# A hybrid attention block on one core: the steps at the seam to the feed-forward part from one table, another block order of the output projection, and local score products over all 128 rows

## The chip, the cores and the metric

The kernel runs on one core of one Trainium2 chip. The metric is the device time of one execution in microseconds (us), as the median of several runs. Lower is better.

## What is computed

One decoder layer on 1024 tokens of width 1024, all in float32. Cut to what matters here:

```python
h = rmsnorm(x, mix_norm_g)
qa, ka, va, q_lat, kv_lat, k_r, g_a, g_b = split(h @ w_in)
o_a = swa_sink_attention(rope(qa), rope(ka), va, sinks)   # 8 heads, 2 kv heads, window 128
o_b = mla_attention(...)                                  # 8 heads, causal, latent q and kv
y = sigmoid(g_a) * (o_a @ w_o_swa) + sigmoid(g_b) * (o_b @ w_o_mla)
x = x + y @ w_out                                         # the output projection
h = rmsnorm(x, ffn_norm_g)
x = x + (silu(h @ w_gate) * (h @ w_up)) @ w_down          # d_ff = 2816
return rmsnorm(x, final_norm_g)
```

## The kernel before

**Products.** Every float32 product is made of three products of a rounded high part and the low rest of each operand (`mm3`, L252 to L258: high by high, high by low, low by high). So each operand is split first: ScalarE copies the high part (`split`, L249), VectorE subtracts it from the source and keeps the rest (L250). The large products use a seven-product block scheme (Strassen-Winograd): the operands are cut into 2 x 2 blocks, some products take sums of blocks, and the results are put together from the seven products. The block sums of weights are made by GpSimd.

**Stages.** The input projection and local (windowed) attention with the gate products between them; latent attention; the gated mix of both (`mix_b`, L1537); the output projection (`X_ORDER`, L1804 to L1870); the gate and up products of the feed-forward part (`Seven`, L783, run 154 times); the down product; the last norm.

**Local scores** (`sw_scores`, L975 to L987). The tile `qs` holds for each of two head pairs and each of two heads 128 rows: 64 rows of the high part of q and 64 rows of its low rest. `khd` holds the keys twice, in rows 0 to 63 and in rows 64 to 127, as a high and as a low tile. A product with the high keys runs over all 128 rows and so adds high and low part of q. A product with the low keys runs over 64 rows alone, rows 0 to 63 for one head (`j = 0`) and rows 64 to 127 for the other (L985). A step has eight such products: two high, two pairs of low ones, two high. There are 16 steps.

**Latent attention** is ordered by a planner (`Plan`, L95) that picks the next step of each engine by estimated times and ranks (`RANK`, L1245).

**The output projection and the seam.** Seven products `q` in the order 1, 2, 6, 7, 5, 4, 3, each over four row blocks `t` of 128 tokens. Products 1, 2, 5, 3 add up in one set of PSUM banks, 6, 7, 4 in another. After each one `xo_done` (L1808) adds the banks to the rows of `x` that are due. Product 4 is the last that rows 0 to 511 (blocks 0 to 3) need, product 3 the last for rows 512 to 1023 (blocks 4 to 7). For each block then follow: the sum of squares (`row_sum`, ScalarE and GpSimd), the scaled row `xn` (`row_norm`, VectorE), eight transposes to the tile `tp` (`next_h`, `to_ps`), and the split tiles of the normed block. The feed-forward part takes them as blocks `b11`, `b21` (from blocks 0 to 3), `b22` (from 4 to 7) and as the block sums `t1` to `t4` (`to_h` L1666, `rest`, `late_split` L1794), each as a high (`t1h`) and a low tile (`t1l`). In `to_h` and `rest` the tile `t` holds two of these sums, and `hraw` the raw blocks and then the other two. GpSimd does one subtraction of `hraw`, the low part of `t3` and the low part of `t4` for each of blocks 4 to 7.

**The feed-forward products** run by pairs `j` of weight columns, products `q`, and matrix `m` ("g" for gate, "u" for up); a list `head` puts (0,1), (0,2), (1,1), (1,2) first, then the products 6, 7, 5, 4, 3 of pair 0 and of pair 1, because 6 and 7 need `t2` and `t3`, 5 needs `t1` and 4 needs `t4`. Each run (`run`, L861) is 12 matmuls of 512 columns. `prep` (L836) splits a weight block into `wl`; `mix` (L822) makes the weight sums `sm` on GpSimd, three operations for each matrix, and `prep` of product 7 one more (`a12 - s1`).

From product 4 of the output projection until 14 weight blocks are prepared (L1844 to L1911) the instructions of PE, VectorE, ScalarE and GpSimd stand in the order of the code; behind that a scheduler orders them. `wd_out` (L1746) makes block sums of `w_down` on GpSimd and stores them, one call for each pair `j`; for j = 0 and 1 it is called after product 5 of that pair.

Of the kernel before, what the change touches and what calls it, by code (L numbers as in the profile page):

```python
# [8 lines left out]
F32 = mybir.dt.float32  # L9
# [169 lines left out]
def hybrid_block_kernel(  # L179
# [603 lines left out]
    class Seven:  # L783


        def __init__(self, pairs, ms, load, done, ahead, load_at, mix_at, head=(), at=None, scale=None, scale_at=(), piece=4):
# [17 lines left out]
            self.piece = piece  # L804
            self.raws, self.sums, self.left, self.acc, self.tmp = {}, {}, {}, {}, {}

# [10 lines left out]
        def part(self, j, m, kh, f):  # L817
            self.load_part(j, kh)
            self.scale_part(j, kh)
            return self.raws[(j, kh)][m][:, :, f]  # L820

        def mix(self, j, eng=None, m=None):  # L822

            for m in self.ms if m is None else (m,):
                if (j, m) in self.sums:
                    continue
                a11, a21, a22 = self.part(j, m, 0, 0), self.part(j, m, 0, 1), self.part(j, m, 1, 1)
                s = self.sums[(j, m)] = U("sm", F32, (P, 2, 4, P))
                eng_, n = (eng, 4) if eng is not None else (nc.gpsimd, self.piece)
                for k in range(0, 4, n):  # L830
                    k = slice(k, k + n)
                    add(s[:, 0, k], a21[:, k], a22[:, k], eng_)
                    sub(s[:, 1, k], s[:, 0, k], a11[:, k], eng_)
                    sub(a21[:, k], a11[:, k], a21[:, k], eng_)

        def prep(self, j, q, m):  # L836
# [5 lines left out]
            if q == 7:  # L842
                a12, s1 = self.part(j, m, 1, 0), self.sums[(j, m)][:, 1]
                for k in range(0, 4, self.piece):
                    k = slice(k, k + self.piece)
                    sub(a12[:, k], a12[:, k], s1[:, k], nc.gpsimd)
# [14 lines left out]
        def run(self):  # L861
# [21 lines left out]
            elif q == 6:  # L883
                add(u2, ps, p1, nc.vector)
            elif q == 7:
                add(u3, ps, p1, nc.vector)
# [9 lines left out]
    def load_gate(j, kh):  # L896
        t = U("wr", F32, (P, 4, 2, P))
# [3 lines left out]
    def scale_gate(j, kh, k, raw):  # L901
        t = raw["g"]
        g = gT[:, 4 * kh + k:4 * kh + k + 1]
        if j == 0:
            nc.vector.tensor_scalar(t[:, k], t[:, k], g, None, op0=ALU.mult)  # L905
        else:
            nc.scalar.activation(t[:, k], t[:, k], AF.Copy, scale=g)
# [67 lines left out]
    def sw_scores(it):  # L975
# [7 lines left out]
        for hp, low in ((0, 0), (0, 1), (1, 1), (1, 0)):  # L983
            for j in range(2):
                r = slice(HD * j, HD * j + HD) if low else slice(0, P)  # L985
                nc.tensor.matmul(scs[j][:, hp, c0:], qs[r, hp, j], khd[g][low][r, kc], start=low == hp,
# [258 lines left out]
    RANK = {'S': -2.38, 'M': -0.6, 'E': -2.86, 'W': -2, 'C': -2, 'V': 3.5, 'O': 1.49, 'A': 2.32, 'Q': -0.9, 'Qm': 2.11, 'Qh': 1.76, 'Ql': 0.5, 'K': -0.3, 'Kh': 0.92, 'Kl': 0.91, 'uh': -1.71, 'ul': -0.83, 'wl': 6.31, 'G': 2.93, 'wh': 0.76, 'bl': 0.9, 'ol': -0.89, 'H': -0.5, 'oh': -0.63}  # L1245
# [279 lines left out]
    proj_steps("oa", 1, NT - 3)  # L1525
# [11 lines left out]
    def mix_b(dc):  # L1537
# [6 lines left out]
        for sh in (1, 0):  # L1544
# [12 lines left out]
    def y_split(q, k):  # L1557
# [4 lines left out]
        src = y_new[0][:, k] if q == 5 else y[k + 4 * (q in (2, 3, 4))][:, half({1: 1, 2: 1, 6: 1, 7: 0, 4: 0, 3: 1}[q])]  # L1562
        split(hi[:, k], lo[:, k], src)

    def y_sums(k):
# [3 lines left out]
        a21, a11, a22, a12 = y[k][:, half(0)], y[k][:, half(1)], y[4 + k][:, half(0)], y[4 + k][:, half(1)]  # L1569
# [83 lines left out]
    raw1 = {}  # L1653
    late = []
# [11 lines left out]
    def to_h(pss, b):  # L1666

        c = b % 4
        if b < 4:
            if b == 0:  # L1670
                new_h("b11")
                new_h("b21")
            raw1[b] = U("hraw", F32, (P, 2, 4, P))
            for kh in range(2):
                split_h(("b11", "b21")[kh], c, pss[kh])
            for kh in range(2):
                nc.scalar.copy(raw1[b][:, kh], pss[kh])
            return
        if b == 4:
            for name in ("b22", "t2", "t3"):  # L1680
                new_h(name)
        r = raw1.pop(c)
        t23 = U("t23", F32, (P, 2, 4, P))
        nc.scalar.copy(t23[:, 1], pss[0])
        sub(r[:, 0], pss[0], r[:, 0], nc.vector)
        sub(t23[:, 0], pss[1], r[:, 0], nc.vector)
        nc.scalar.copy(hq["t2"][0][:, :, blk(c)], t23[:, 0])
        sub(r[:, 1], r[:, 1], t23[:, 0], nc.gpsimd)
        late.append((c, r))

        def rest():
            sub(t23[:, 1], pss[1], t23[:, 1], nc.vector)
            nc.scalar.copy(hq["b22"][0][:, :, blk(c)], pss[1])
            nc.scalar.copy(hq["t3"][0][:, :, blk(c)], t23[:, 1])
            for name, src, eng in (("t2", t23[:, 0], nc.vector), ("b22", pss[1], nc.vector),
                                   ("t3", t23[:, 1], nc.gpsimd)):
                hi, lo = hq[name]
                sub(lo[:, :, blk(c)], src, hi[:, :, blk(c)].bitcast(F32), eng)

        return rest  # L1700

# [3 lines left out]
    def load_w(j, kh):  # L1705
        if j == 0:
            t = [U("wr", F32, (P, 4, 2, P)) for _ in range(2)]
        else:
            v = V("wr", F32, (P, 2, 4, 2, P))
# [5 lines left out]
    def ffn_done(j, m, ps, f, sh, other):  # L1715
# [3 lines left out]
        if other is not None:  # L1719
            add(other, ps, other, nc.vector)  # L1720
# [3 lines left out]
        else:  # L1724
# [4 lines left out]
                {(1, 6): [("load", 2, 0)], (1, 7): [("load", 2, 1)], (1, 5): [("mix", 2)]})  # L1729
# [64 lines left out]
    def late_split(c):  # L1794
        r = late[c][1]
        for i, name in ((0, "t1"), (1, "t4")):
            if c == 0:
                new_h(name)
            split_h(name, c, r[:, i], (nc.vector, nc.gpsimd)[i])
        late[c] = None  # L1800
# [4 lines left out]
    xns = []  # L1805
    rests = []
# [301 lines left out]
```

## Time and profile before

| what | us |
|---|---|
| median of 3 runs | 1347.29 (1346.72 to 1348.11) |
| the profiled execution | 1347.01, of which 1345.2 from the first to the last instruction (the span) |
| TensorE (PE) busy | 1325.4 |
| VectorE (DVE) busy | 927.2 |
| ScalarE (ACT) busy | 653.5 |
| GpSimd (POOL) busy | 591.5 |

A profile lists for each engine when every instruction started and how long it took. PE's matmuls are pipelined: a record of one 512-column product lasts 0.39 us, but the next one starts earlier. Rows of "windows" give, for a stretch of the span, the busy time of PE, of PE's weight loads, of DVE, ACT and POOL with the number of instructions, then the clock that PE was granted (1.00 is full) and the share and rate of the DMA engines. A row of "waits" gives who waited for whom: microseconds in total, how often, the longest.

### The profile page before, as it was taken

Reading aid. Unit: us, or ns where it says so; the run is one execution under the profiler, and the core shown is the slowest. Engines: PE = TensorE matmul, PEld = TensorE weight load, DVE = VectorE, ACT = ScalarE, POOL = GpSimd, SP = SyncE. Lnnn points to the kernel's source line nnn. Section 1 sums busy time; section 2 is a strip of 40 time slices with the busy share of each in tenths; the row PEclk is TensorE's granted clock in tenths of the full one; section 3 lists DMA queues with packets and bytes.
Section 4 is the critical chain, followed back from the end, with each engine's and each line's share of the span. In section 5 each row is a group of like instructions: output and inputs, shape, how many; then the busy total and the mean of one; then the engine's idle time right before and its main releaser. Section 6 shows DMA issues by size and latency. Waiting matters only on the chain. (4 is left out here: it accounts for less than half of the span.)

```text
span 1345.2 us, 18917 instructions
## 1 busy us (share of the span) xinstructions
PE 1325.4 (99%) x6552; PEld 1112.4 (83%) x6552; DVE 927.2 (69%) x1565; ACT 653.5 (49%) x1317; POOL 591.5 (44%) x598
## 2 busy tenths in 40 slices
PE   9999999999999999999998999999999999999997
PEld 6899878878888889888886788888888888888886
DVE  7868767776787786488779675666665654674862
ACT  7433767655577787534365233232222232644352
POOL 1116545454054567230056865756666541022521
PEclk9999999999999999999999999999999999999999
DMA  9454322334200111987042353544443425996504
GB/s 367 159 184 156 116 100 89 99 118 161 90 13 1 47 45 48 328 247 223 1 188 78 132 182 133 208 168 180 166 154 150 164 95 189 368 379 250 172 15 142
DMA packets 78239, 205.39 MB, mean 153 GB/s; under 512 B 8768, under 2 KB 15424, under 8 KB 77504
## 3 DMA queue, kind: packets, MB, share of 16 engines
q1 hardware_dynamic: 76848, 199.99, 42.4%
q0 software_dynamic: 1152, 4.19, 1.6%
q8 instruction: 52, 0.85, 0.3%
q14 instruction: 43, 0.35, 0.1%
q10 hardware_dynamic: 144, 0.00, 0.0%
HBM read 141.24 MB, written 59.77 MB: 149 GB/s over the span
## 5 line engine op out<-in xcount | busy, mean ns | idle before, releaser
L250 DVE TENSOR_TENSOR wl<-wr,wl 128x512 fp32r<-128x512 f32 x150 | 153.4, 1044 | 74.2 <-ACT wl L249 73.9
L250 DVE TENSOR_TENSOR lrv<-lr,lrv 128x1024 fp32r<-128x1024 f32 x77 | 105.1, 1397 | 51.5 <-ACT lrv L249 50.2
L249 ACT CAST lrv<-lr 128x1024 fp32r<-128x1024 f32 x77 | 80.1, 1052 | 96.7 <-PE fd L258 53.9
L256 PE MATMUL fd<-lrv 128*128 128x512 f32 x308 | 119.8, 389 | 0.0
L257 PE MATMUL fd<-lrv 128*128 128x512 f32 x308 | 119.8, 389 | 0.0
L258 PE MATMUL fd<-lrv 128*128 128x512 f32 x308 | 119.8, 389 | 0.0
L261 POOL TENSOR_TENSOR wr<-wr,sm 128x512 f32<-128x512 f32 (+1 forms) x38 | 46.5, 1232 | 116.2 <-DVE wl L250 110.1
L249 ACT CAST wl<-wr 128x512 fp32r<-128x512 f32 x150 | 87.2, 622 | 2.6 <-DVE wr L905 2.0
L250 DVE TENSOR_TENSOR wl<-sm,wl 128x512 fp32r<-128x512 f32 x60 | 53.9, 924 | 45.2 <-ACT wl L249 45.1
L1299 POOL TENSOR_SCALAR p<-p,denb 128x384 f32<-128x384 f32 (+3 forms) x64 | 48.0, 753 | 63.5 <-DVE denb L1295 52.3
L384 POOL TENSOR_SCALAR ms<-ss 128x1 f32<-128x1 f32 x32 | 9.8, 305 | 141.8 <-ACT xn L1820 64.1
L256 PEld LDWEIGHTS fd<-lrv 128*128 128x128 f32 x308 | 57.8, 188 | 12.1
L257 PEld LDWEIGHTS fd<-lrv 128*128 128x128 f32 x308 | 57.8, 188 | 12.0
L258 PEld LDWEIGHTS fd<-lrv 128*128 128x128 f32 x308 | 57.8, 188 | 11.9
L1290 ACT ACTIVATE p<-scb,nmb 128x384 f32<-128x384 f32 (+3 forms) x64 | 47.7, 746 | 23.4 <-DVE nmb L1285 17.4
L1723 ACT ACTIVATE act<-sm 128x512 f32<-128x512 f32 x11 | 7.0, 633 | 105.9 <-DVE sm L264 105.9
L261 DVE TENSOR_TENSOR ptl<-pTb,pth 128x512 fp32r<-128x512 f32 (+2 forms) x96 | 51.1, 551 | 8.1 <-ACT pth L1326 7.4
L1285 DVE CUSTOM_DVE_ANT_0 scb<-scb,mask 128x384 f32<-128x384 f32 (+3 forms) x64 | 48.5, 759 | 8.9 <-PE scb L1272 8.5
L1723 ACT ACTIVATE act<-pu 128x512 f32<-128x512 f32 x22 | 13.9, 633 | 74.4 <-DVE pu L264 74.4
L258 PE MATMUL fa<-t1h,wl 128*128 128x512 f32 x120 | 47.4, 397 | 2.6 <-DVE wl L250 2.6
L258 PE MATMUL fb<-t3h,wl 128*128 128x512 f32 x120 | 47.2, 394 | 1.7 <-DVE wl L250 1.7
L256 PE MATMUL fa<-t1h,wl 128*128 128x512 f32 x120 | 47.9, 399 | 0.0
(363 smaller groups left out, 4341.6 us busy)
## 6 DMA issues: line engine op xcount, KB each, us to landing
lr<-la_d SPq DMA_DIRECT2D x77, 256.0 KB, 5.4
wr<-in_w_gate_dram SPq DMA_DIRECT2D x22, 512.0 KB, 4.3
wr<-in_w_up_dram SPq DMA_DIRECT2D x22, 512.0 KB, 5.3
wd<-in_w_down_dram SPq DMA_DIRECT2D x22, 512.0 KB, 6.8
rb_d<-wd SPq DMA_DIRECT2D x22, 512.0 KB, 2.6
la_d<-sd SPq DMA_DIRECT2D x22, 512.0 KB, 5.4
lr<-rb_d SPq DMA_DIRECT2D x44, 256.0 KB, 5.4
lr<-in_w_down_dram SPq DMA_DIRECT2D x33, 256.0 KB, 5.3
```

Of the source, the lines that this page charges most:

```text
L249: nc.scalar.copy(hi, src)
L250: (eng or nc.vector).tensor_tensor(lo, src, hi.bitcast(F32), op=ALU.subtract)
L256: nc.tensor.matmul(ps, ah, bh, start=first and i == 0, stop=False, skip_group_check=go_on)
L257: nc.tensor.matmul(ps, ah, bl, start=False, stop=False, skip_group_check=go_on)
L258: nc.tensor.matmul(ps, al, bh, start=False, stop=last and i == n - 1, skip_group_check=go_on)
L261: eng.tensor_tensor(out, a, b, op=ALU.subtract)
L384: nc.gpsimd.tensor_scalar(ms, ss, 1.0 / width, EPS, op0=ALU.mult, op1=ALU.add)
L1285: nc.vector.tensor_tensor_reduce(s_, s_, m_, 1.0, -NEG, op0=ALU.add, op1=ALU.min, accum_out=nm)
L1290: nc.scalar.activation(p_, s_, AF.Exp, scale=-1.0, bias=t_.pop(("nm", key)), accum_out=den)
L1299: nc.gpsimd.tensor_scalar(p[:, 0:w], p[:, 0:w], den, 0.0, op0=ALU.mult, op1=ALU.add)
L1723: nc.scalar.activation(dst, src, AF.Silu)
```

## The change

1. **Local scores.** The low products run over all 128 rows too, so that each of the eight products of a step has the same form. They add the product of the low rests, which was left out before.
2. **Output projection.** The order of products is 1, 2, 6, 5, 3, 7, 4, and the halves of rows change roles (also in `y_split`, `y_sums`, `mix_b`): product 3 is now the last that blocks 0 to 3 need, two products before the end, and product 4 the last for blocks 4 to 7. The order of code (not of the scheduler) holds from product 3 on.
3. **The seam from a table.** `SEAM` lists the steps as words: `x30` is product 3 on row block 0, `y` the next operand split of the projection, `s0`, `n0`, `T0` sum of squares, scaled row and transposes of block 0, `h`, `c` and the letters and digits after `T4` single instructions of `to_h` and `rest`, `t`, `v` the splits of `t1` and `t4`, `p` one weight split, `f` one feed-forward run, `m`, `M` weight sums, `D` the DMA of point 4. All subtractions of `hraw`, `t3` and `t4` are on VectorE.
4. **Weight sums.** Signs are turned (`plus=True`), so that the sums of weights are additions. For pair 0 the sum that `prep` of product 7 made on GpSimd (one operation for each matrix) is made by a DMA that adds (`mix_sum(0, 2)`, issued by GpSimd); `mix_load` and the other steps of `mix_sum` are not called.
5. **Layout.** The weight tiles hold the two column blocks of a pair one behind the other, so that a slice of 512 is contiguous (`pairs`, `load_gate`, `load_w`).
6. **Small things.** Ranks for two kinds of steps in the planner of latent attention (`L`, `T`) and one due time; `mix_b` takes the halves in the other order; `wd_out` of pairs 0 and 1 is called after product 5 of pairs 2 and 3.

```diff
     class Seven:
...
-                    sub(s[:, 1, k], s[:, 0, k], a11[:, k], eng_)
-                    sub(a21[:, k], a11[:, k], a21[:, k], eng_)
+                    op(s[:, 1, k], s[:, 0, k], a11[:, k], eng_)
+                    op(a21[:, k], a11[:, k], a21[:, k], eng_)
+        def mix_sum(self, j, step):
+            def plus(dst, src):
+                nc.gpsimd.dma_start(dst, src, accum_op=ALU.add)
...
+                else:
+                    plus(self.part(j, m, 1, 0), s[:, 1])
...
-            if q == 7:
+            if q == 7 and j not in self.by_dma:
...
-                r = slice(HD * j, HD * j + HD) if low else slice(0, P)
-                nc.tensor.matmul(scs[j][:, hp, c0:], qs[r, hp, j], khd[g][low][r, kc], start=low == hp,
+                nc.tensor.matmul(scs[j][:, hp, c0:], qs[:, hp, j], khd[g][low][:, kc], start=low == hp,
                                  stop=low != hp)
...
-    proj_steps("oa", 1, NT - 3)
+    proj_steps("oa", 1, NT - 4)
...
-        for sh in (1, 0):
+        for sh in range(2):
...
+        elif what == "3":
+            sub(t23[c][:, 1], t23[c][:, 1], pss[1], nc.vector)
+        elif what == "i":
+            add(raw1[c][:, 1], raw1[c][:, 1], t23[c][:, 0], nc.vector)
...
+        elif what == "H":
+            sub(hq["t3"][1][:, :, blk(c)], t23[c][:, 1], hq["t3"][0][:, :, blk(c)].bitcast(F32), nc.vector)
+        elif what in "tv":
...
+            split_h(name, c, raw1[c][:, what == "v"], (nc.vector, nc.vector)[what == "v"])
...
-    X_ORDER = (1, 2, 6, 7, 5, 4, 3)
+    X_ORDER = (1, 2, 6, 5, 3, 7, 4)
...
+    SEAM = ("y x30 y s0 n0 x31 y x32 s1 n1 s2 x33 y s3 T0 n2 h0 x70 y m0 c0 T1 n3 x71 h1 c1 T2 x72 h2 c2 m1 "
...
-        if (q, m) == (5 if j < 2 else 2, "u"):
-            if j < HF - 1:
-                wd_out(j)
+        if (q, m) == (2, "u") and 2 <= j < HF - 1:
+            wd_out(j)
+        if (q, m) == (5, "u") and j in (2, 3):
+            wd_out(j - 2)
...
-        return m.reshape(2, 4, P, 2, n, P).transpose(4, 0, 2, 1, 3, 5)
+        return m.reshape(2, 4, P, 2, n, P).transpose(4, 0, 2, 3, 1, 5)
```

**Where instructions move.** On DVE, the splits of `t1` stand beside the first feed-forward runs that need `t2` and `t3` (`fb`: the bank of products 6, 7, 4; `pu`: partial results; `sm`, `wr`: weight sums and weights; `wl`: split weights; `act`: the activations). Before, DVE's rows there were:

```order
L1725 TENSOR_TENSOR act_7879<-fa_7836,act_7879 128x512
L250 TENSOR_TENSOR t1l_7904<-hraw_7491,t1h_7903 128x4x128
L264 TENSOR_TENSOR pu_7710<-fb_7911,pu_7710 128x512
L250 TENSOR_TENSOR t1l_7904<-hraw_7550,t1h_7903 128x4x128
L250 TENSOR_TENSOR wl_7930<-wr_7327,wl_7930 128x512
L264 TENSOR_TENSOR pu_7730<-fb_7933,pu_7730 128x512
L250 TENSOR_TENSOR t1l_7904<-hraw_7595,t1h_7903 128x4x128
L250 TENSOR_TENSOR wl_7952<-wr_7328,wl_7952 128x512
L264 TENSOR_TENSOR sm_7448<-fb_7911,pu_7710 128x512
L250 TENSOR_TENSOR t1l_7904<-hraw_7637,t1h_7903 128x4x128
```

With the change, the same engine at the same place:

```order
L250 TENSOR_TENSOR t1l_7906<-hraw_7472,t1h_7905 128x4x128
L250 TENSOR_TENSOR wl_7909<-wr_7253,wl_7909 128x512
L261 TENSOR_TENSOR pu_7708<-pu_7708,fb_7912 128x512
L250 TENSOR_TENSOR t4l_7927<-hraw_7534,t4h_7926 128x4x128
L250 TENSOR_TENSOR t1l_7906<-hraw_7504,t1h_7905 128x4x128
L250 TENSOR_TENSOR t4l_7927<-hraw_7504,t4h_7926 128x4x128
L250 TENSOR_TENSOR t4l_7927<-hraw_7472,t4h_7926 128x4x128
L261 TENSOR_TENSOR pu_7733<-pu_7733,fb_7936 128x512
L250 TENSOR_TENSOR wl_7950<-wr_7254,wl_7950 128x512
L250 TENSOR_TENSOR t1l_7906<-hraw_7534,t1h_7905 128x4x128
L250 TENSOR_TENSOR wl_7955<-sm_7468,wl_7955 128x512
```

The four low parts of `t4` stand between those of `t1` now; before they were GpSimd's. From the transposes of block 4 to the last `t1l` DVE has 39 instructions before and 50 with the change.

On GpSimd (POOL), before, from the first low part of `t3` on:

```order
L261 TENSOR_TENSOR t3l_7681<-t_1432_7682,t3h_7680 128x4x128
L261 TENSOR_TENSOR t3l_7681<-t_1445_7745,t3h_7680 128x4x128
L261 TENSOR_TENSOR hraw_7595<-hraw_7595,t_1453_7821 128x512
L261 TENSOR_TENSOR t3l_7681<-t_1453_7821,t3h_7680 128x4x128
L261 TENSOR_TENSOR hraw_7637<-hraw_7637,t_1459_7861 128x512
L261 TENSOR_TENSOR t3l_7681<-t_1459_7861,t3h_7680 128x4x128
L250 TENSOR_TENSOR t4l_7908<-hraw_7491,t4h_7907 128x4x128
L250 TENSOR_TENSOR t4l_7908<-hraw_7550,t4h_7907 128x4x128
L261 TENSOR_TENSOR wr_7352<-wr_7352,sm_7448 128x4x128
```

With the change, behind the last small operation of the norms:

```order
L387 TENSOR_TENSOR rstd_7668<-ms_7666,neg_half 128x1
L850 DMA wr_7335<-sm_7468 128x512
L850 DMA wr_7336<-sm_7537 128x512
L264 TENSOR_TENSOR sm_7997<-wr_7574,wr_7603 128x512
L264 TENSOR_TENSOR sm_7997<-sm_7997,wr_7574 128x512
L264 TENSOR_TENSOR wr_7574<-wr_7574 128x4x128
```

GpSimd has no block work left at the seam: the two adding DMAs of point 4 and then at once the weight sums of pair 1.

More of the change, by code (lines that the diff above doesn't have):

```diff
@@ L1674, in to_h @@
             for kh in range(2):
                 split_h(("b11", "b21")[kh], c, pss[kh])
+        elif what == "c":
+            raw1[c] = U("hraw", F32, (P, 2, 4, P))
             for kh in range(2):
[L1677 to L1680, printed above, removed]
-                new_h(name)
[L1682 to L1685, printed above, removed]
```

234 lines of the change are left out of this document (118 added, 116 removed), and 3 rows, old and new, of the table SEAM.

## The prediction

> **What bounds the kernel now.** I read the page first. PE is busy for nearly the whole span:
>
> ```profile
> PE 1325.4 (99%) x6552; PEld 1112.4 (83%) x6552; DVE 927.2 (69%) x1565; ACT 653.5 (49%) x1317; POOL 591.5 (44%) x598
> ```
>
> So the end is set by PE's stream, and there are two ways to gain: fewer or shorter matmuls, or less idle time between them. The windows by stage say where it idles (local attention, latent attention, mix and projection, the seam, the rest; first number PE's busy time, then PEld, DVE, ACT, POOL, the clock):
>
> ```profile
> 100.00:325.00 225.00, 221.30 (x1197) 187.18 (x1196) 168.55 (x420) 140.63 (x390) 123.53 (x191) 1.00 0.35 114
> 325.00:545.00 220.00, 219.56 (x1343) 192.85 (x1342) 159.64 (x380) 153.93 (x338) 102.73 (x106) 1.00 0.18 59
> 545.00:690.00 145.00, 145.00 (x655) 120.40 (x655) 109.75 (x146) 67.92 (x93) 31.02 (x27) 1.00 0.63 200
> 690.00:750.00 60.00, 53.86 (x242) 42.48 (x242) 51.20 (x59) 35.26 (x66) 40.15 (x33) 0.97 0.21 78
> 750.00:1345.00 595.00, 588.09 (x2595) 486.64 (x2593) 363.21 (x392) 203.87 (x313) 276.67 (x204) 1.00 0.52 184
> ```
>
> The seam lacks 6.1 us of 60 and a part of the clock. The projection lacks nothing, latent attention 0.4. The last row also gives the pitch of a 512-column product: 588.09 / 2595 = 0.227 us. PE's waits in 700 to 750 us name the releasers:
>
> ```profile
> PE fa L258 <- DVE wl L250: 2.6, 1, 2.6
> PE fb L258 <- DVE wl L250: 1.7, 2, 1.3
> PE fa L256 <- ACT pu L882: 1.1, 1, 1.1
> PE fb L257 <- DVE t2l L261: 0.8, 1, 0.8
> ```
>
> Together 6.2 us. Smaller windows show DVE filling up, then POOL, and then the clock falling:
>
> ```profile
> 720.00:730.00 10.00, 8.80 (x36) 6.79 (x37) 9.62 (x12) 8.16 (x17) 6.87 (x6) 1.00 0.18 56
> 730.00:740.00 10.00, 7.85 (x32) 5.48 (x30) 10.00 (x9) 2.71 (x6) 9.92 (x7) 1.00 0.52 180
> 740.00:747.00 7.00, 4.94 (x15) 3.89 (x16) 4.39 (x5) 0.35 (x1) 7.00 (x5) 0.76 0.00 1
> ```
>
> In 730 to 740 DVE is busy throughout, with nine instructions. At 0.76 over 7 us the clock costs 7 x 0.24 = 1.7 us. DVE's groups in 700 to 746 say why so few fit:
>
> ```profile
> L250 DVE TENSOR_TENSOR wl<-wr,wl 128x512 fp32r<-128x512 f32 x8 | 10.3, 1311 | 0.3 <-ACT wl L249 0.3
> L250 DVE TENSOR_TENSOR wl<-sm,wl 128x512 fp32r<-128x512 f32 x4 | 5.4, 1369 | 0.2 <-ACT wl L249 0.2
> L250 DVE TENSOR_TENSOR t1l<-hraw,t1h 128x512 fp32r<-128x512 f32 x4 | 4.7, 1183 | 0.0
> L261 DVE TENSOR_TENSOR t2l<-t,t2h 128x512 fp32r<-128x512 f32 x4 | 4.6, 1150 | 0.2
> L261 DVE TENSOR_TENSOR b22l<-tp,b22h 128x512 fp32r<-128x512 f32 x4 | 2.7, 680 | 0.4 <-ACT b22h L1693 0.4
> ...
> L250 POOL TENSOR_TENSOR t4l<-hraw,t4h 128x512 fp32r<-128x512 f32 x4 | 6.6, 1673 | 0.3 <-ACT t4h L249 0.3
> L261 POOL TENSOR_TENSOR hraw<-hraw,t 128x512 f32<-128x512 f32 x4 | 6.1, 1530 | 10.4 <-DVE t L261 10.4
> L261 POOL TENSOR_TENSOR t3l<-t,t3h 128x512 fp32r<-128x512 f32 x4 | 5.2, 1298 | 3.3 <-ACT t3h L1694 2.9 <-PE tp L1662 0.4
> ```
>
> All have the same size. With a source in PSUM (`tp`) DVE takes 0.68 us. With both sources in SBUF it takes 1.15 to 1.37 while POOL works, but no more than 0.69 when POOL is still:
>
> ```profile
> 695.24 0.69 DVE L250 TENSOR_TENSOR wl<-wr,wl 128x512 fp32r<-128x512 f32 x1 [0.62 <-ACT wl L249]
> 695.85 0.68 DVE L264 TENSOR_TENSOR x<-x,xo 128x512 f32<-128x512 f32 x1
> ```
>
> These two rows also show that the next instruction starts 0.61 us after such a one, so 0.60 is what each takes of DVE's time. Over the 20 SBUF instructions POOL's work costs DVE 8 x 0.62 + 4 x 0.68 + 4 x 0.49 + 4 x 0.46 = 11.5 us. That is where the seam's waits come from.
>
> **Part 1, local scores.** One step of eight products at 168 us, from the timeline (start, duration, rows x columns; x2 are two in one row, which together last no longer than one):
>
> ```profile
> 168.23 0.28 PE L986 MATMUL sc<-khd,qs 128*128 128x256 f32 x1
> 168.35 0.28 PE L986 MATMUL sc<-khd,qs 128*128 128x256 f32 x1
> 168.56 0.39 PE L986 MATMUL sc<-khd,qs 64*128 64x256 f32 x2
> 168.78 0.28 PE L986 MATMUL sc<-khd,qs 64*128 64x256 f32 x2
> 168.99 0.39 PE L986 MATMUL sc<-khd,qs 128*128 128x256 f32 x1
> 169.22 0.28 PE L986 MATMUL sc<-khd,qs 128*128 128x256 f32 x1
> 169.33 0.39 PE L256 MATMUL fb<-t2h,wl 128*128 128x512 f32 x1
> ...
> 69.00 0.29 PE L256 MATMUL qa<-wv,hh 128*128 128x256 f32 x1
> 71.40 0.29 PE L258 MATMUL qa<-wv,hl 128*128 128x256 f32 x1
> ```
>
> The step lasts 169.33 - 168.23 = 1.10 us. The two low pairs do run side by side, but the change from 128 rows to 64 and back costs: 0.21, 0.22, 0.21 and 0.23 us stand where 0.12 would. The products of `qa` (the same 256 columns, 128 rows, new weights each time) follow each other at (71.40 - 69.00) / 20 = 0.12 us. Eight of these are 0.96, so a step gains 0.14. Fourteen of the 16 steps have 256 columns; the two first of a head group have 128 and I give them nothing. Sum: 14 x 0.14 = **2.0 us less**, on PE, where nothing covers it. The bounds: 0, if the changes between products stay dear, and 2.3, if the two narrow steps gain as well. PE's few waits in this stage (225.00 - 221.30) hang on DVE and ACT work of the same loop, which moves along.
>
> The Trainium skill speaks against this part: "TensorE: Matmul & The Clock Gate", Part 3 (Packing small matmuls), says that products on separate row groups run at once, some 4 ns apart, so that packing two of them nearly halves their time. The rows agree that pairs run at once and differ on the gain: a pair stands for 0.22, two products of `qa` for 0.24, and the two changes of form cost 0.1 each. By that rule a step before would take four slots and two pairs of slots in one, 6 x 0.12 = 0.72, and the change would add 0.24 to each step.
>
> **Part 2, the seam.** The change takes off POOL four `hraw`, four `t3l`, four `t4l` and two `wr<-wr,sm` operations; the first twelve go to DVE, the two become DMAs. It adds 12 x 0.60 = 7.2 us to DVE if nothing stretches them. I compare both engines between the transposes of block 4 and the first product that reads `t1`. PE has the same there in both programs: 32 transposes and 12 runs of 12 products. Eight transposes pass in 0.79:
>
> ```profile
> 172.09 1.03 PE L1019 MATMUL pT<-ident,pe 128*128 128x128 f32 x8
> 172.88 0.48 PE L256 MATMUL fa<-hh,wl 128*128 128x512 f32 x1
> ...
> 730.09 1.77 DVE L250 TENSOR_TENSOR wl<-wr,wl 128x512 fp32r<-128x512 f32 x1
> ```
>
> So PE has 4 x 0.79 + 144 x 0.227 = 35.9 us of work there. (The last row is for below.) DVE before: 37 instructions of 512 and two of 1024 (1.2 each), 24.6 us, and 16 of them have both sources in SBUF, stretched by 0.58 on average (11.5 / 20): 33.9. That would just fit into 35.9, but the blocks come one behind the other, through POOL and ACT and back, and PE waits 6.2. DVE after: 49 and one, 30.6 us. That fits with 5.3 to spare, as long as POOL is still, and no block passes through POOL any more. And one pass of the projection (48 products, 10.9 us) now lies between the end of blocks 0 to 3 and that of 4 to 7, in which their `h` and `c` steps are done.
>
> POOL is not still to the end: behind the two DMAs its next work is the weight sums of pair 1, with no block work ahead of them, so they start when their tiles are free, and that can be beside the last `t1l`. Of DVE's last seven instructions before the first `t1` product five have both sources in SBUF; between 1.31 (the mean) and 1.77 (the row at 730.09) they lose 0.6 to 1.1 each, 3.1 to 5.4 of the 5.3. Ahead stand 0.8 for the transposes of block 4, and a scaled row that is late for its transposes in the passes 3 and 7 can cost some tenths. So PE is left with waits between 0 and, if the handing on between engines costs half of what it did, 3.5; I take 2.0, nearer to the sum. The waits go from 6.2 to 2.0, **4.2 us less** (bounds 2.7 and 6.2).
>
> The clock fell behind the wait of 2.6. The waits of 1.1 and 1.3 left it at 1.00 (720 to 740). With 2.0 left, in two or three pieces, it should stay, **1.7 us less** (bounds 0 and 1.7). A single wait over 2 us would be a risk. The Trainium skill ("TensorE: Matmul & The Clock Gate", Part 1) says that the half clock comes after an idle window of some 3.4 us; here it came with 2.6 at most in one piece, so the trace is stricter than that.
>
> The DMAs that add:
>
> ```profile
> 574.03 1.99 POOL L1591 DMA_DIRECT2D wo<-wo  x2
> wo<-wo POOLq DMA_DIRECT2D x6, 512.0 KB, 9.6
> ```
>
> POOL is held 2 us by two of them and they land after 9.6 us (for twice these bytes). What waits: the sum of product 7, which overwrites the `sm` they read, on DVE, with the last `t1l` queued behind. Five runs, 5 x 2.73 = 13.6 us, lie between. Nothing, with 2 us to spare.
>
> **Part 3, the rest at nothing.** Layout: `wl<-wr` at 0.69 reads its slice in four pieces already and takes no longer than `x<-x,xo` at 0.68. Ranks in latent attention: 0.4 us of idle is all there is to win; I allow 1 us for a new wait, since a run of PE's rows changes order. Projection: PE lacks nothing in 545 to 690, and DVE has 109.75 of 145. `wd_out` of pairs 0 and 1: eight POOL operations go from right behind the seam to pairs 2 and 3, beside 276.67 of 595 us of POOL; without that room the down product would wait, 400 us later. SP's queue gets the same loads.
>
> **Sum.** Against the profiled execution (1347.01, span 1345.2): 2.0 + 4.2 + 1.7 = 7.9 less. The median of the runs is 0.3 above it, so 1347.3 - 7.9 = **1339.4**.
>
> **Rivals.**
> 1. *DVE stays the bound.* The twelve operations and POOL's weight sums meet. With all 28 SBUF instructions stretched by 0.58 DVE needs 30.6 + 16.2 = 46.8 us against 35.9. Two thirds of that stretch leave a wait of 5.5, and the low clock: 2.0 + 0.7 less, 1344.6. For it speaks that DVE has no idle time in 730 to 740; against it that POOL has 8 operations for 22 then (12 go to DVE, 2 become DMAs).
> 2. *Packing pays.* The 0.21 to 0.23 are hold-ups of another kind that stay, and giving up the pairs adds 2 x 0.12 in each of 16 steps, 3.8. With the seam's gain of 5.9: 1345.2. The Trainium skill's Part 3, above, is the rule behind it. Against it: the same `qa` products without any hold-up.
> 3. *Slower.* A 128-row product behind another one of the same step costs what the seventh does (169.22 - 168.99 = 0.23): eight take 1.84, not 1.10, 0.74 x 14 = 10.3 more. It decides from 0.137 a product for this part (1.10 / 8) and from 0.19 for the whole (5.9 / 112 more). 1347.3 + 10.3 - 5.9 = 1351.7. For it: that row; against it: `qa` at 0.12, with new weights each time too.
> 4. *It does not do what it says.* New waits in latent attention, or of transposes on scaled rows in passes 3 and 7, eat what the seam gains, and part 1 alone is left: 1345.3.
>
> **How the numbers follow.** The forecast gets 0.78, rival 1 0.10, the others 0.04 each. The forecast's own range goes from 1336 (2.3 + 6.2 + 1.7 and a spare us) to 1344.6 (0 + 2.7 + 0); the upper end would need all three at their worst, so most of it lies below 1343. The range of 8 in 10 takes in both ends and part of rival 1: 1335.8 to 1344.5. A measurement can tell 0.2%, 2.7 us, from no change: faster means below 1344.6. That is nearly all of the forecast (0.77) and half of rival 1 (0.05): 0.82. Slower is rival 3, 0.04; the same is the rest, 0.14.
>
> **What would show it.** Right: a score step of 0.96 us in one form; no `fb` wait on `wl`, at most one wait near the first `t1` product, below 2.5 us; SBUF splits at 0.69 until POOL starts on pair 1; clock 1.00 throughout. Wrong: steps over 1.1 us; POOL's sums next to `t2l` and `t3l`; a low clock behind the seam; a wait on the adding DMA; PE idle in 325 to 690.

## The result, and the profile after

The changed kernel takes **1336.42 us** (median of 4 runs, 1336.13 to 1337.95) against 1347.01 for the kernel before (4 runs). The ratio is 0.9923, with a 95% interval of 0.9906 to 0.9940. The forecast was 1339.4, in a range of 1335.8 to 1344.5. The profiled execution has a span of 1334.4 us, 10.8 less than before. Of the executions behind the runs below, one of e1 took 1645 us at a mean clock of 0.75; it is in no ratio.

The page's busy times of the changed kernel:

```profile
PE 1319.4 (99%) x6552; PEld 1113.8 (83%) x6552; DVE 932.6 (70%) x1577; ACT 652.3 (49%) x1317; POOL 573.4 (43%) x586
```

PE's waits in 690 to 760 us:

```profile
PE fa L257 <- DVE t1l L250: 1.6, 1, 1.6
```

PE is busy 6.0 us less, for 10.8 us of span. One wait is left of five, and it is at the first `t1` product. The windows of the seam, in the columns used above:

```profile
700.00:710.00 10.00, 10.00 (x54) 8.45 (x53) 9.86 (x16) 6.90 (x12) 0.00 (x0) 1.00 0.09 17
710.00:720.00 10.00, 10.00 (x49) 8.33 (x48) 9.89 (x17) 7.79 (x15) 0.00 (x0) 1.00 0.07 27
720.00:730.00 10.00, 9.90 (x44) 7.88 (x42) 9.85 (x13) 6.05 (x12) 5.60 (x4) 1.00 0.37 131
730.00:740.00 10.00, 8.52 (x37) 7.05 (x38) 8.81 (x8) 1.09 (x3) 7.67 (x5) 1.00 0.01 2
```

From 700 to 720 POOL does nothing, DVE passes 33 instructions and PE has no gap. POOL comes back at 724 us. The clock stays at 1.00.

Three tiles mark the stages: `lT` is the first of latent attention, `xo` of the output projection, `fd` of the down product. Their rows show the shortest, median and longest duration and the first and the last start. First the kernel before, then the changed one:

```profile
L1122 PE MATMUL lT<-ident,lat x40: 270/272/329, 328.8 to 341.9; 128*128 128x128 f32 x40
L256 PE MATMUL xo<-woh,yh x112: 389/389/478, 616.2 to 695.3; 128*128 128x512 f32 x112
L256 PE MATMUL fd<-lrv x308: 389/389/389, 1128.5 to 1337.3; 128*128 128x512 f32 x154
```

```profile
L1149 PE MATMUL lT<-ident,lat x40: 270/272/328, 326.9 to 339.9; 128*128 128x128 f32 x40
L256 PE MATMUL xo<-woh,yh x112: 389/389/478, 613.5 to 692.6; 128*128 128x512 f32 x112
L256 PE MATMUL fd<-lrv x308: 389/389/390, 1117.6 to 1326.4; 128*128 128x512 f32 x154
```

Up to latent attention about 2.0 us are gained (328.8 to 326.9), in latent attention 0.7 to 0.8 (287.4 to 286.6), from the projection to the down product 8.2 (512.3 to 504.1), behind that nothing (208.8 both times). The first of these is the least certain: in eight profiles of kernels that are the same up to `lT` (the changed one, e3 to e7, e10, e12) `lT` starts anywhere from 326.9 to 329.1.

### The profile page after: what moved, and what is told of

Same layout as the page of the kernel before. It is cut to its first block, busy times and chain, and to the rows that moved or that the text cites. A ratio compares the mean times of both kernels' runs of the same rounds, so it can differ in the third digit from the quotient of the medians.

```text
span 1334.4 us, 18920 instructions
## 1 busy us (share of the span) xinstructions
PE 1319.4 (99%) x6552; PEld 1113.8 (83%) x6552; DVE 932.6 (70%) x1577; ACT 652.3 (49%) x1317; POOL 573.4 (43%) x586
## 4 chain that ended last, share of the span: by engine, by line
PE 83%; DVE 3%; ACT 1%; POOL 1%; issue 0%; POOLq 0%; DVEq 0%; ACTq 0%
PE fa L257 7%; PE fa L258 7%; PE fa L256 7%; PE fb L258 6%; PE fb L257 6%; PE fb L256 6%; PE fd L256 5%; PE fd L258 5%; PE fd L257 5%; PE pTb L1342 2%; PE xo L258 2%; PE xo L257 2%; PE xo L256 2%; PE ob L1380 1%; PE scb L1297 1%; PE ob L1379 1%
## 5 line engine op out<-in xcount | busy, mean ns | idle before, releaser
L264 POOL TENSOR_TENSOR wr<-wr,sm 128x512 f32<-128x512 f32 x20 | 30.1, 1507 | 96.6 <-DVE wl L250 96.6
L264 POOL TENSOR_TENSOR sm<-wr,wr 128x512 f32<-128x512 f32 (+1 forms) x36 | 40.5, 1130 | 34.6 <-DMA wr<-in_w_gate_dram 31.3
L257 PE MATMUL fa<-t1l,wl 128*128 128x512 f32 x120 | 46.9, 391 | 1.6 <-DVE t1l L250 1.6
L256 PE MATMUL fb<-t2h,wl 128*128 128x512 f32 x120 | 47.4, 395 | 0.0
```

The lines of the kernel that those rows point to most:

```text
L256: nc.tensor.matmul(ps, ah, bh, start=first and i == 0, stop=False, skip_group_check=go_on)
L257: nc.tensor.matmul(ps, ah, bl, start=False, stop=False, skip_group_check=go_on)
L264: eng.tensor_tensor(out, a, b, op=ALU.add)
```

## The experiments

"Hold" below is a version that the first results led to. Each time is a median; the ratio is to the kernel before on the same chip. The chips differ: beside e1 to e4 the kernel before took 1346.66, beside e5 to e8 1346.64, beside e9 to e12 1346.75, against 1347.01 beside the changed kernel. So differences of up to 0.4 us between rows of different chips say nothing.

| run | what | us | ratio (95%) |
|---|---|---|---|
| | the changed kernel | 1336.42 | 0.9923 (0.9906 to 0.9940) |
| e1 | before, 128-row low products only | 1345.45 | 0.9991 (0.9982 to 1.0001) |
| e2 | before, the twelve operations on DVE only | 1352.56 | 1.0040 (1.0028 to 1.0053) |
| e3 | changed, the twelve back on POOL | 1342.53 | 0.9969 (0.9958 to 0.9981) |
| e4 | changed, no adding DMA | 1337.16 | 0.9926 (0.9913 to 0.9940) |
| e5 | changed, old ranks | 1337.51 | 0.9935 (0.9923 to 0.9948) |
| e6 | changed, `wd_out` early | 1336.53 | 0.9928 (0.9914 to 0.9941) |
| e7 | changed, with the hold | 1334.73 | 0.9911 (0.9898 to 0.9925) |
| e8 | before, half of each pair | 1346.29 (one run) | |
| e9 | e2 with the hold | 1349.14 | 1.0015 (1.0006 to 1.0024) |
| e10 | e7, blocks 0 to 3 a pass later | 1338.16 | 0.9937 (0.9924 to 0.9949) |
| e11 | e7, 64-row low products | 1336.64 | 0.9925 (0.9911 to 0.9938) |
| e12 | e7, no adding DMA | 1334.57 | 0.9911 (0.9897 to 0.9924) |

### e1 and e11: the local score products

```diff
-                r = slice(HD * j, HD * j + HD) if low else slice(0, P)
-                nc.tensor.matmul(scs[j][:, hp, c0:], qs[r, hp, j], khd[g][low][r, kc], start=low == hp,
+                nc.tensor.matmul(scs[j][:, hp, c0:], qs[:, hp, j], khd[g][low][:, kc], start=low == hp,
```

e1 makes this edit in the kernel before; e11 takes it back in e7.

> The kernel before with one line of the change alone: the low score products run over all 128 rows. My theory: the 16 score steps take what they take in the changed kernel (16.8 us together, 0.95 for most) in place of 18.4, so 1.65 less: 1345.4 of 1347.0; the seam keeps its 6.2 us of waits and its low clock. The wait of 1.0 us for qn at 118 us, which the changed kernel lacks, comes before the first score step; if it is chance, either profile can show it (then up to 1344.4), if it belongs to another part of the change it stays. Rival (the pairs pay): within 0.3 of 1347.0, or above it.

> The version with the hold (1334.7, its runs within 0.2 of each other) with the low score products on 64 rows again. Theory: the 16 steps take 18.4 in place of 16.8 us: 1334.73 + 1.65 = 1336.4. Rival (waits of the same loop take up part of it): 1335 to 1335.7.

The step that was shown in the prediction, in the changed kernel:

```profile
167.42 1.12 PE L1013 MATMUL sc<-khd,qs 128*128 128x256 f32 x8
168.38 0.40 PE L256 MATMUL fb<-t2h,wl 128*128 128x512 f32 x1
```

It takes 168.38 - 167.42 = 0.96, as the prediction had it, for 1.10. Added up from start to start, the 16 steps take 18.42 us before and 16.77 after, 1.65 less; in the traces of e11 and e7 it is 18.46 and 16.57. e1 alone gains 1.2 us, with an interval that reaches just past no change; taking the edit out of e7 costs 1.9 (e11's runs lie between 1335.2 and 1337.6, e7's between 1334.7 and 1334.9). Both agree with the steps. In e1 the seam's waits are the old ones, and the wait for `qn` at 118 us isn't there. It is 0.2 in e6 and e8 and 0.6 in e11, and 0 in e2, e5 and e7: the 1.0 us of the one profile of before is chance and no part of the change.

### e8: what a pair costs

```diff
             for j in range(2):
+                if low and j == 1:
+                    continue
```

(The start and stop marks of `j = 1` move to its high products.)

> The kernel before, with one of the two 64-row low products of each pair left out (that part of the scores isn't computed). It asks what a pair's 0.22 us are made of. Theory (the two run at once, the time is the change of form): a step with six products still takes 1.10 us. Rival (the two go one after the other at 0.11 each, though their starts are recorded 4 ns apart): 1.10 - 0.22 = 0.88. In the time of the kernel, 0 against 16 x 0.22 = 3.5 us less.

```profile
168.78 1.26 PE L988 MATMUL sc<-khd,qs 128*128 128x256 f32 x6
169.88 0.40 PE L256 MATMUL fb<-t2h,wl 128*128 128x512 f32 x1
```

Six products take 169.88 - 168.78 = 1.10, as eight did. So the second product of a pair is free: the two run at once. What the step pays besides is (1.10 - 6 x 0.12) / 4 = 0.1 at each of the four places that the prediction named. Only two of these are changes of form, so a change costs about 0.2: the product behind it and the next one each come 0.1 late. The weight loads (PEld) go with that:

```profile
169.11 0.18 PEld L988 LDWEIGHTS sc<-khd,qs 64*128 64x128 f32 x1
169.11 0.38 PE L988 MATMUL sc<-khd,qs 64*128 64x256 f32 x1
169.77 0.19 PEld L256 LDWEIGHTS fb<-t2h,wl 128*128 128x128 f32 x1
```

Inside a form a load starts 0.11 ahead of its product (169.77 for 169.88). Behind a change it starts only with its product (both at 169.11), and the product after that is 0.1 late as well. What holds the load back is not shown. Two changes cost 0.38 and two pairs save 0.24, so the 64-row form loses 0.14. The rule of the Trainium skill ("TensorE: Matmul & The Clock Gate", Part 3) is right about the pair; it gives no price for the change to 64 rows and back.

### e2 and e3: who does the twelve operations

e2 gives the four `hraw`, four `t3l` and four `t4l` operations to DVE in the old order, as shown here; e3 gives them back to POOL in the new one (steps `i`, `H` and `v` of the table).

```diff
-        sub(r[:, 1], r[:, 1], t23[:, 0], nc.gpsimd)
+        sub(r[:, 1], r[:, 1], t23[:, 0], nc.vector)
...
-                                   ("t3", t23[:, 1], nc.gpsimd)):
+                                   ("t3", t23[:, 1], nc.vector)):
...
-            split_h(name, c, r[:, i], (nc.vector, nc.gpsimd)[i])
+            split_h(name, c, r[:, i], (nc.vector, nc.vector)[i])
```

> The kernel before, with only the twelve operations (four hraw subtractions, four t3l, four t4l) given to VectorE, in the old order of code. Theory (GpSimd's neighbouring work is what stretches VectorE): the SBUF instructions fall from 1.15 to 1.37 us to about 0.69 until the weight sums begin, the waits in 700 to 750 us go from 6.2 to 2 to 3 us and the low clock goes: 1347.0 - 5 = 1342. Rival (the order is what counts): the blocks still come late, one behind the other, the waits stay at 5 or more, 1345.5 to 1348.

> The changed kernel, with the same twelve operations given back to GpSimd, the table's order kept. Theory (GpSimd's neighbouring work stretches VectorE): the SBUF instructions rise to 1.2 us or more in 705 to 730, the waits go from 1.6 to 4 to 7 us, 1336.4 + 3 to 7 = 1339 to 1343. Rival (the order is what counts): at most 1 us more, 1336.4 to 1337.4.

| | twelve on POOL | twelve on DVE |
|---|---|---|
| old order | 1346.66 | 1352.56 |
| new order, with the rest of the change | 1342.53 | 1336.42 |

The time of e3 came out as expected, that of e2 against both expectations: the move alone makes the old order 5.9 us **slower**. (Of the 5.8 between the two profiles 3.9 lie between the projection and the down product; 1.0 lies ahead of the projection, where the programs are the same, and 0.9 behind PE's last product, which stays unexplained.) DVE's SBUF instructions did fall to 0.68 there, between 710 and 731 us. But PE's waits in 700 to 750 read:

```profile
PE fa L256 <- ACT pu L882: 3.2, 2, 2.9
PE fb L258 <- DVE wl L250: 2.9, 2, 2.5
PE fa L258 <- DVE wl L250: 2.1, 1, 2.1
```

The first one was 1.1 before. ACT's timeline of e2 shows why it grew (in brackets the idle time before, and who ended it):

```profile
720.35 0.62 ACT L1687 CAST t2h<-t 128x512 fp32r<-128x512 f32 x1 [2.03 <-DVE t L261]
721.68 0.58 ACT L1693 CAST b22h<-tp 128x512 fp32r<-128x512 f32 x1 [0.71 <-DVE t L261]
722.16 0.62 ACT L1694 CAST t3h<-t 128x512 fp32r<-128x512 f32 x1
722.68 0.62 ACT L249 CAST wl<-sm 128x512 fp32r<-128x512 f32 x1
723.20 0.59 ACT L882 COPY pu<-fa 128x512 f32<-128x512 f32 x1
```

The copy `pu<-fa`, which frees PE's bank, stands in ACT's queue behind the block's `t2h`, `b22h` and `t3h`, and those wait for DVE. In the old order a block's steps stand in a row, so each instruction that DVE gets for the block before delays this copy. POOL had done these twelve beside it. This is read from the queues; no run moved the copy alone. The new order spreads a block's steps between the runs, and with the same twelve on DVE PE has the one wait of 1.6.

In e3 the largest part of the loss hangs on one instruction of DVE's timeline:

```profile
720.93 6.86 DVE L250 TENSOR_TENSOR wl<-sm,wl 128x512 fp32r<-128x512 f32 x1
```

POOL's timeline beside it:

```profile
720.41 1.83 POOL L850 DMA_DIRECT2D wr<-sm  x2
721.61 1.95 POOL L261 TENSOR_TENSOR t3l<-t,t3h 128x512 fp32r<-128x512 f32 x1
722.96 4.28 POOL L250 TENSOR_TENSOR t4l<-hraw,t4h 128x512 fp32r<-128x512 f32 x3
```

PE's longest wait, 3.5 us, is for that `wl`. DVE's `wl<-sm` is held from 720.93 until POOL has ended four operations in a row (722.96 + 4.28 = 727.24) and then takes its usual 0.6. The Trainium skill ("SBUF — State Buffer", Who interferes with whom) says that a VectorE instruction with two SBUF inputs and a GpSimd instruction that reads SBUF exclude each other, and that the second to start waits for the first. The 1.77 of the other profiles fits one such wait of 1.1; here it went on over four. Why it did is not shown; the two DMA issues of POOL right ahead (720.41) are one thing that differs. Behind the wait of 3.5 the clock stood at 0.50 for 6.8 us, which costs some 3 us more.

### e4, e12 and e6: the parts put at nothing

```diff
-                by_dma=(0,))
+                by_dma=())
...
-        if (q, m) == (2, "u") and 2 <= j < HF - 1:
-            wd_out(j)
-        if (q, m) == (5, "u") and j in (2, 3):
-            wd_out(j - 2)
+        if (q, m) == (5 if j < 2 else 2, "u"):
+            if j < HF - 1:
+                wd_out(j)
```

The first is e4 (in the changed kernel) and e12 (in e7; both also leave the word `D` out of the table), the second e6.

> The changed kernel, with the sum for product 7 of pair 0 on GpSimd (two operations) in place of the two adding DMAs. Theory: two GpSimd operations of about 1.3 us stretch two to four VectorE instructions by 0.5 each, so 1 to 2 us of what VectorE had to spare is gone and the wait at the first t1 product grows from 1.6 to 2 to 3.5: 1337 to 1338.5. Rival (the DMAs matter little): 1336.4 within 0.4.

> The version with the hold, with the sum for product 7 on GpSimd in place of the adding DMAs. In the changed kernel this made no difference to any wait. Theory (without the hold a wait of 1.6 hid it; now VectorE has under 1 us to spare): two GpSimd operations at some 695 to 705 us stretch two or three instructions by 0.5, and a wait of up to 1 us may come at t1: 1334.7 to 1335.7. Rival (it lies where VectorE has slack): 1334.7 within 0.2.

> The changed kernel with the block sums of w_down of pairs 0 and 1 at their old place, behind product 5 of these pairs. Theory (put at nothing in the prediction): PE has no waits behind the seam in either place, so 1336.4 within 0.5. Rival (GpSimd's eight operations right behind the seam stretch VectorE's splits there): a wait of 1 to 3 us appears between 735 and 760: 1337.4 to 1339.4.

The time of e4 lies where its theory had it, but not for the theory's reason: e4 has the same single wait of 1.6 as the changed kernel, and in its profile the seam takes the same time; it is 1.0 us later already at the projection, ahead of which the two programs are the same. e12 takes 1334.57, e7 1334.73. The adding DMAs gain nothing and cost nothing here: POOL does these two operations at some 700 us, before it could hurt. e6 takes 1336.53 and shows no wait but that of 1.6 up to 790 us; its profile loses 0.4 us at 753, in pieces too short for the view of waits. Both terms were rightly put at nothing, to within some tenths.

### e5: the ranks

The entries `'L': -0.93` and `'T': 0.7` leave `RANK`, and:

```diff
-    proj_steps("oa", 1, NT - 4)
+    proj_steps("oa", 1, NT - 3)
```

> The changed kernel with the old ranks and due time in latent attention. In the changed kernel's trace the stretch from the first q product to the first output-projection product is 0.7 us shorter than before (264.3 for 265.0), most of it between score products. Theory (the ranks do it): the 0.7 comes back: 1336.4 + 0.7 = 1337.1, and the stretch is 265.0 again. Rival (it came with the layout or by chance): the stretch stays at 264.3.

```profile
L1149 PE MATMUL lT<-ident,lat x40: 270/272/329, 329.1 to 342.2; 128*128 128x128 f32 x40
L256 PE MATMUL xo<-woh,yh x112: 389/389/478, 616.4 to 695.5; 128*128 128x512 f32 x112
```

Latent attention takes 616.4 - 329.1 = 287.3 us again, and the time is 1.1 us longer. The ranks do it: all six profiles with the old ranks (the kernel before, e1, e2, e5, e8, e9) have 287.2 to 287.3 there, and all eight with the new ones 286.6. PE had no idle time there to win: the ranks change the sequence of products, and by their starts the score products (`scb`) follow each other 0.9 us closer in sum, the transposes of the weights (`pTb`) 0.4 less so. That it is the changes of form which become fewer was not tried.

### e7: what makes the last wait

```diff
         elif what == "M":
+            hold = tiny("hold")
+            nc.gpsimd.tensor_scalar(hold, hq["t1"][1][:, 0, blk(3)][:, 0:1].bitcast(F32), 1.0, 0.0, op0=ALU.mult,
+                                    op1=ALU.add)
             ffn.mix(1)
```

> The changed kernel, with GpSimd held by one small operation that reads the last low part of t1, so that the weight sums of pair 1 start behind it and not beside it (at 724 us now). Theory (these sums stretch VectorE's last splits and so make the wait): the five instructions that take 1.15 to 1.77 us before the last t1l take 0.69, the wait of 1.6 at the first t1 product goes, with the 0.1 behind it: 1336.4 - 1.7 = 1334.7. Rival (VectorE is late anyway, or the next splits, of t4 and of weights, get the stretch and PE waits for them): a wait of 1 to 2 us stays, there or within the next 10 us: 1336 to 1337.

DVE's last instructions before the `t1` products, first in the changed kernel, then in e7 (start, duration):

```profile
725.16 1.19 DVE L250 TENSOR_TENSOR wl<-wr,wl 128x512 fp32r<-128x512 f32 x1
726.28 1.77 DVE L250 TENSOR_TENSOR t1l<-hraw,t1h 128x512 fp32r<-128x512 f32 x1
727.97 1.77 DVE L250 TENSOR_TENSOR wl<-sm,wl 128x512 fp32r<-128x512 f32 x1
729.67 0.68 DVE L261 TENSOR_TENSOR sm<-fb,pu 128x512 f32<-128x512 f32 x1
730.27 1.15 DVE L250 TENSOR_TENSOR t1l<-hraw,t1h 128x512 fp32r<-128x512 f32 x1
```

```profile
725.63 0.68 DVE L250 TENSOR_TENSOR wl<-wr,wl 128x512 fp32r<-128x512 f32 x1
726.23 0.68 DVE L250 TENSOR_TENSOR t1l<-hraw,t1h 128x512 fp32r<-128x512 f32 x1
726.83 0.68 DVE L250 TENSOR_TENSOR wl<-sm,wl 128x512 fp32r<-128x512 f32 x1
727.45 0.69 DVE L261 TENSOR_TENSOR sm<-fb,pu 128x512 f32<-128x512 f32 x1
728.06 0.68 DVE L250 TENSOR_TENSOR t1l<-hraw,t1h 128x512 fp32r<-128x512 f32 x1
```

The row with a source in PSUM (`fb`) is 0.68 in both. PE's busy time in e7's windows is full:

```profile
720.00:730.00 10.00, 10.00 (x46) 8.28 (x45) 9.85 (x18) 6.52 (x13) 1.17 (x2) 1.00 0.39 131
730.00:740.00 10.00, 10.00 (x46) 8.29 (x45) 8.73 (x9) 3.00 (x6) 9.92 (x7) 1.00 0.01 2
```

The wait is gone, no other came up to 790 us, and the time is 1334.73, as expected: **the best version here** (e12, at 1334.57, can't be told from it). The sums still stretch DVE, up to 1.79 us, from 730 to 743, where PE doesn't wait for it.

### e9 and e10: the order of code

e9 adds the hold to e2. e10 moves the words for blocks 0 to 3 in e7's table:

```diff
-    SEAM = ("y x30 y s0 n0 x31 y x32 s1 n1 s2 x33 y s3 T0 n2 h0 x70 y m0 c0 T1 n3 x71 h1 c1 T2 x72 h2 c2 m1 "
-            "T3 x73 h3 p c3 x40 s4 p p x41 n4 s5 x42 s6 n5 x43 s7 n6 T4
...
+    SEAM = ("y x30 y x31 y x32 x33 y x70 y s0 n0 x71 s1 n1 x72 s2 n2 m0 x73 s3 T0 h0 p c0 x40 T1 n3 h1 c1 s4 p p x41 T2 n4 s5 "
+            "h2 c2 m1 x42 T3 s6 n5 h3 c3 x43 s7 n6 T4
...
```

> The old order with the twelve operations on VectorE (as in the run that took 1352.6) and GpSimd's weight sums of pair 1 held until the last low part of t1 is done. In that run the first wait of 2.9 us (PE for a bank that ScalarE copies to pu, behind the block's t2h and t3h) with its low clock costs 5, and the later waits with theirs, beside GpSimd's sums, 7.5. Theory (the sums make the second part, the order of code the first): the second part goes, the first stays: 1352.6 - 7 = 1345 to 1346. Rival (the old order makes both): 1350 or more.

> The changed kernel with the hold of 1334.7, but the table's steps for blocks 0 to 3 moved about one pass later, as they stood before: scaled rows, transposes and h and c steps during product 4 where product 7 is now. Theory (the pass in between gives VectorE the room): VectorE has some 11 us of work more in the last pass than it can do, transposes and splits come late, waits of 2 to 5 us return between 682 and 735: 1337 to 1340. Rival (engine and table are enough): 1334.7 within 0.5.

PE's waits of e9, then those of e10 over 0.3 us (660 to 790 us):

```profile
PE fa L256 <- ACT pu L882: 3.3, 2, 3.0
PE fb L256 <- DVE pu L264: 2.4, 1, 2.4
PE fa L258 <- DVE wl L250: 0.9, 1, 0.9
PE fb L257 <- DVE t2l L261: 0.7, 1, 0.7
PE fb L258 <- DVE wl L250: 0.2, 1, 0.2
```

```profile
PE fa L256 <- ACT b11h L249: 0.8, 1, 0.8
PE fa L257 <- DVE b11l L250: 0.7, 1, 0.7
```

e9 lies between the expectations (1349.14). Its profile is the fastest of its eleven executions (1346.74, at a mean clock of 0.999, where nine of them have 0.995 or 0.996), so it shows the waits of e9 but not the clock of most. The wait behind `pu` stayed at 3.0, as the theory said, and the late waits on `wl` fell from 5.0 to 1.1. But 2.4 us came back at 760 us, for a `pu` of DVE, whose instructions beside the held sums take up to 1.78 until 755 us. In the old order neither the engine nor the hold makes it faster than before. e10 costs 3.4 us more than e7, inside what was expected: the blocks are done just too late for the first runs, on ACT and DVE alike. So in this table the pass of the projection between the two halves is worth about 3.4 of the seam's gain; another late order was not tried.

## Why the prediction was right

- **Part 1, 2.0 less.** The mechanism was right, a step takes 0.96. The 16 steps gave 1.65: twelve of the 14 wide ones gain 0.15 each and the two narrow ones, put at nothing, 0.07 each, but the two at 145 and 156 us take 0.25 longer together. Rival 2 failed on its price, not on its mechanism: pairs do run at once (e8), and a change of form costs 0.2, not the 0.1 that the prediction gave it.
- **The seam's waits, 6.2 to 2.0.** Measured: 6.2 to 1.6, in one piece, at the product and for the tile that was named, and for the reason given (e7). Of DVE's last instructions four were stretched and lost 0.5 + 1.1 + 1.1 + 0.5 = 3.2 us, the low end of the 3.1 to 5.4.
- **The step that was mis-sized** is "4.2 us less" for the waits: it took a wait to cost what the view of waits shows. This is the last wait of the changed kernel on PE's timeline:

```profile
729.51 0.39 PE L256 MATMUL fa<-t1h,wl 128*128 128x512 f32 x1
731.48 0.50 PE L257 MATMUL fa<-t1l,wl 128*128 128x512 f32 x1 [1.58 <-DVE t1l L250]
731.82 0.39 PE L258 MATMUL fa<-t1h,wl 128*128 128x512 f32 x1
```

  Two products take 731.82 - 729.51 = 2.31 where 0.45 would do: 1.85 for a wait of 1.58. Of the 0.27 more, 0.16 is the tail of the product ahead, which counts as busy (0.39 for a pitch of 0.23), and 0.11 the slower start behind. Before there were five waits and some hold-ups too short to show as waits. Counted from start to start, against 0.227 a product and 0.1 a transpose, PE lost 10.7 us from the first product of the projection through 26 feed-forward runs, and loses 2.5 after the change. The 8.2 are 4.6 of waits, 1.6 of low clock (eight products at 0.43) and 2.0 of this kind, which the sum had left out.
- **The clock, 1.7 less.** Right in this profile, 1.6, but it is no fixed price. In e1 the same wait of 2.6 left the clock alone. The traces give a reason that fits all of them. In each, every change of the clock up to the end of PE's work stands a whole multiple of 3.413 us behind the first one (in the kernel before at 5.83, then 216 and 217 multiples behind it, at 743.10 and 746.52). So an execution can be cut into stretches of that length. Here are the stretch with the wait and the next one in the kernel before, then the two that share the wait in e1:

```profile
739.69:743.10 3.41, 1.04 (x5) 0.87 (x6) 3.41 (x4) 0.00 (x0) 3.41 (x3) 1.00 0.02 8
743.10:746.52 3.42, 3.42 (x10) 2.64 (x9) 1.26 (x2) 0.00 (x0) 3.42 (x4) 0.50 0.00 0
```

```profile
736.97:740.39 3.42, 2.25 (x10) 1.50 (x8) 3.42 (x3) 0.00 (x0) 3.34 (x3) 1.00 0.51 161
740.39:743.80 3.41, 2.01 (x9) 1.67 (x10) 3.04 (x3) 0.00 (x0) 3.41 (x3) 1.00 0.00 0
```

  In the 14 profiles the clock falls four times between the start and the end of the work, each time right behind a stretch in which PE was busy for 1.08 us or less (0.52 and 0.95 in e2, 1.04 before, 1.08 in e3), and never behind one with 1.56 (e8) or more. In the kernel before, 2.37 of the wait of 2.56 fell into one stretch; in e1 it was split, 1.17 and 1.40. By these figures what counts is how much of a wait one stretch takes, and where the stretches lie differs from one execution to the next. The prediction's "the trace is stricter than that" took the wait for what counts. A wait of 1.6 leaves PE busy for 1.8 us of a stretch, so after the change the clock is safe by these figures. Of the 16 runs of the kernel before beside e1 three have a mean clock of 0.999 and take 1344.6 to 1345.5; the seven at 0.997 take 1345.9 to 1348.0. So most of them, not all, seem to have the fall.
- **Part 3, nothing.** Right for the adding DMAs, `wd_out` and the projection. Wrong for the ranks: 0.7 us, without any idle time to win (e5). "0.4 us of idle is all there is to win" looked at gaps alone, and the pitch of products depends on their sequence too.
- **Why both halves of part 2 were needed** the prediction had not asked. It added the twelve operations to DVE at 0.60 each and took the order as given. e2 shows that they alone lose 5.9 us. e3 shows that without them the rest of the change gains 4.1, of which the steps and the ranks are 2.4. So at the seam the new order, with the layout and the signs of the weight sums that no run takes apart from it, is worth under 2 alone, and the order and the twelve together 8.2.
- Rival 1 named the right pair, POOL's sums and DVE, but 1.6 us of wait, not 5.5. Rivals 3 and 4 didn't come.

The time came out within 0.6 us of the low end of the range. The prediction had reached that end another way, with no wait left at all, 2.3 for part 1 and a spare us. Measured, a wait of 1.6 stayed, and 2.7 us came from two things that the sum had at nothing, the hidden part of the waits and the ranks. So the mechanisms of parts 1 and 2 were right, and that the range was wide enough for the rest was in part luck.

The sum then reads: 1.65 for the steps, 0.7 for the ranks, 8.2 for the seam, 10.55 in all; the medians differ by 10.6. That the two agree so closely is chance too, since the stages ahead of `lT` alone vary by 2.3 from one execution to the next. The 0.3 that is left of the profiles' 10.8 is the start, the wait for `qn` and some longer waits in local attention against each other.

## What to carry to other kernels

- A wait on PE costs its length and about 0.27 us more here; short waits in a row are worth more than the view of waits says. Products that alternate between 128 and 64 rows pay about 0.2 at each change here, so a smaller product of another form can cost as much as a full one.
- Work moved to an engine pays only where the order gives it room: look for what stands behind it in the queues, the copy that frees a bank above all.
- Where DVE is the tight engine, keep POOL's large operations away from its last instructions before the product that waits; one small operation that depends on the right tile does it.

## What the runs showed of the hardware

- A 512-column DVE instruction with both sources in SBUF took 0.67 to 0.69 us with POOL still. From 560 us to the down product it took up to 1.86 beside POOL's 512-column operations, 2.9 beside one of 1024 columns (at 571 us in the kernel before), and once, in e3, 6.86, held over four POOL operations in a row; elsewhere the durations fit a wait for one. What makes the difference stays open. With one source in PSUM it took 0.67 to 0.69 throughout.
- Up to the end of PE's work the granted clock changed only at whole multiples of 3.413 us from its first change, in all 14 profiles. It fell to 0.50 behind a stretch of that length in which PE was busy for 1.08 us or less, and stayed at 1.00 with 1.56 or more; it came back after one stretch, or after two behind the wait of 3.5 (e3). The waits behind which it fell were of 2.5 to 3.5 us; 2.6 in e1 and e8 and 3.0 in e9's profile, each shared by two stretches, left it at 1.00. The Trainium skill ("TensorE: Matmul & The Clock Gate", Part 1) names an idle window of some 3.4 us; the length agrees, but the window need not be idle throughout.
- Of two 64-row products on the two halves of the rows the second took no time of its own (1.10 us for a step with and without it). A change between 128 and 64 rows cost about 0.2 us, in two pieces of 0.1.
